# Up projection of a hybrid decoder layer: where the split weights of three of seven products begin in their buffers

## The chip, the cores and the metric

The kernel runs on one core of a Trainium2 chip. The metric is the device time of one execution in microseconds; lower is better. Runs of the kernel before stand beside runs of the changed one.

## The reference

One decoder layer: token mixing (gated linear attention and differential attention) and a gated MLP with a short causal convolution, each with an RMSNorm before and after. What matters here is the first product of the MLP, `h @ w_ffn_in`, with 512 tokens, 2048 inputs and 2 x 5632 outputs, all in float32:

```python
def conv_ffn(h, w_ffn_in, conv_w, conv_b, w_ffn_out):
    S = h.shape[1]
    up = h @ w_ffn_in
    a, b = up[..., :D_FF], up[..., D_FF:]
    a_pad = jnp.pad(a, ((0, 0), (CONV_W - 1, 0), (0, 0)))
    a = (conv_w[0] * a_pad[:, 0:S] + conv_w[1] * a_pad[:, 1:S + 1]
         + conv_w[2] * a_pad[:, 2:S + 2] + conv_b)
    return (jax.nn.gelu(a, approximate=True) * b) @ w_ffn_out
```

## The kernel before

**Split products.** A float32 factor is split into a high part (a copy in the type float32r, on the scalar engine, L130) and a low part (the rest, by a subtraction on the vector engine, L131). Each product is then three matmuls: high weights by high tokens, high by low, low by high. `ah` and `al` hold the token operand's two parts; `whi` and `wlo` hold those of a granule of weights of 1024 numbers in each partition.

**Where a granule begins.** `halves()` takes the two parts from buffers of 1024 + 64 numbers, three in rotation for each part, and returns 1024 of them, from `place_w[0]` on: 0, or 16 numbers, which are 64 bytes. All tiles that TensorE reads here (`ah`, `al`, the sums below, `whi`, `wlo`, and the spare buffers `xhi`, `xlo`) begin at whole multiples of 128 bytes, and the matmuls step through them in pieces of 128 numbers, which are 512 bytes. So the place of an operand within 128 bytes is 0, but for weights where `place_w[0]` is 16: there it is 64.

**The stages.** The input projections and the attention heads come first, then the output projection of the mixer and the change to the MLP (`to_ffn`), which already does the first columns of the up projection (`mm_t`, L166 to L168) with half the tokens (256 columns) at a time: its `weights_f` sets `place_w[0]` to 16 for weights in `whi` and `wlo`, and 0 for those in the spare buffers. Then the rest of the up projection and the down projection run as fast matrix multiplications by blocks, with seven products for each 2x2 block of blocks in place of eight.

**The up projection.** It has 20 units: 10 groups of 512 columns in each of the two branches. A unit (`up_unit`) makes seven products, called `x0`, `z0`, `y0`, `z1`, `x1`, `y1`, `y2` by the PSUM chain that they add to, and each takes one token operand: `a11`, `s5`, `s2`, `s3`, `a12`, `s7`, `a22` in this order. `a11`, `a12`, `s7` and `a22` are four quarters of `ah` and `al` (`s7` takes the place of the quarter that is not needed any more): the four token operands. `s5`, `s2` and `s3` are tiles of their own: the three sums. `Unit.run` does one product: two granules, each split by `granule`, and then `up_prods`, which for each of two pieces of 128 columns and four pieces of 128 inputs makes the three matmuls of L920, L921 and L922, with 128x128 weights as the stationary operand and 256 token columns (two runs of 128) as the moving one. So a granule is 24 matmuls, a product 48, a unit 336, and the projection 6720. In the loop over units the next unit's `x0` stands ahead of this one's `y2`, so that in the order of the program a run of three products on sums (144 matmuls) is followed by a run of four on token operands (192 matmuls).

The down projection uses the same class with `a == 2` and the place 0; there the tokens are the stationary operand (`down_prods`).

What sets the order is the order written out in the loop over units, with a scheduler that places the instructions of each engine; TensorE works its queue in order.

Of the kernel before, what the change touches and what calls it, by code (L numbers as in the profile page):

```python
# [35 lines left out]
def hybrid_layer(ctx: ExitStack, tc: tile.TileContext, x, attn_pre_norm, w_in, w_alpha_up, b_alpha,  # L36
# [69 lines left out]
    place_w = [0]  # L106
# [14 lines left out]
    def granule(src, a, raw=None, spare=None, hl=None):  # L121
        if raw is None:
            raw = load(src, a)
        if hl is not None:
            hi, lo = hl[:, 0, :], hl[:, 1, :]
        elif spare:
            hi, lo = spare_halves(spare)
        else:
            hi, lo = halves()
        act(hi, raw, AF.Copy)  # L130
        tt(lo, raw, hi.bitcast(F32), ALU.subtract)  # L131
        r = "p (a b) -> p a b"
        return hi.rearrange(r, a=a), lo.rearrange(r, a=a)
# [718 lines left out]
    class Unit:  # L852
# [4 lines left out]
        def run(self, seg, op, raws):  # L857
            c = seg[0]
            if seg[1] == "0":
                self.banks[c] = self.chain(c)  # L860
            for g in range(2):
                turn[0] += 1
                place_w[0] = 16 if self.a == 4 else 0
                hl = granule(None, self.a, raws[g], spare=extra[0] and turn[0] % 4 == 0)
                self.prods(self.banks[c], op, g, hl, seg[1] == "0")

# [354 lines left out]
```

## Time and profile before

| what | value |
|---|---|
| three runs | 2157.59, 2170.23, 2169.51 us |
| their median | 2169.51 us |
| the profiled execution | 2165.04 us |
| its span, first to last instruction | 2163.3 us |
| granted clock of TensorE, mean | 0.998 |
| stage of the up projection, us from the span's start | 926.8 to 1723.1 |

The profiled execution's own time is 1.7 us over its span. In the rows of groups, "xN | busy, mean ns" gives the number of instructions, the time in which at least one of them ran, and the mean length of one. Matmuls overlap, so the mean length of one is longer than the distance between their starts. A row of the matmuls in order of time begins with the start and the length in us. In the rows by stage a pair such as "795.71 (x6746)" is an engine's busy time and the number of its instructions that ran in the stretch, those that began before it among them.

### The profile page before, as it was taken

To read this page: it belongs to the slowest core of one execution; us is meant where nothing else is said; L and a number is where in the kernel's file an instruction comes from. 1 tells how busy PE (TensorE), PEld (TensorE's weight loads), DVE (VectorE), ACT (ScalarE), POOL (GpSimd) and SP (SyncE) were. 2 spreads that over 40 slices of the span, in tenths; PEclk is the share of its full clock that TensorE was granted. 3 is DMA by queue.
4 is the path that set the end of the run, shared out by engine and by line. 5 is a ranking of instruction groups with operands and counts; after the bars stand their busy time and mean duration, and the time that the engine had idled before them with its cause. 6 is when DMAs were issued, how large, how long until landed. Compare 5 with 4: busy or idle time off the path is not lost.

```text
span 2163.3 us, 31876 instructions
## 1 busy us (share of the span) xinstructions
PE 2133.1 (99%) x13009; PEld 1902.4 (88%) x13009; DVE 1418.1 (66%) x1722; ACT 901.7 (42%) x1162; POOL 204.9 (9%) x245
## 2 busy tenths in 40 slices
PE   7999999999999999999999999999999999999997
PEld 6878888888888889899999999999999978887886
DVE  5345553444444236787777677786777787888987
ACT  4233332333333234344444444543544555443533
POOL 1000000000000000011101101111111011111101
PEclk9999999999999999999999999999999999999999
DMA  6322222223224344455666657657667688577663
GB/s 212 104 69 78 78 73 84 69 78 87 78 88 166 98 136 170 132 127 136 161 163 154 159 147 180 157 129 184 147 143 184 182 243 217 166 193 177 158 173 136
DMA packets 218472, 303.83 MB, mean 140 GB/s; under 512 B 11777, under 2 KB 155573, under 8 KB 216405
## 3 DMA queue, kind: packets, MB, share of 16 engines
q1 hardware_dynamic: 165204, 238.87, 33.1%
q0 software_dynamic: 53120, 62.92, 18.9%
q8 instruction: 102, 1.67, 0.3%
q14 instruction: 46, 0.37, 0.0%
HBM read 273.97 MB, written 27.79 MB: 139 GB/s over the span
## 4 chain that ended last, share of the span: by engine, by line
PE 62%; issue 29%; POOL 3%; DVE 2%; DMA 2%; ACT 1%; SPq 0%; POOLq 0%; DVEq 0%; ACTq 0%
PE bank L184 6%; PE bank L185 6%; PE bank L186 6%; PE bank L920 5%; PE bank L922 5%; PE bank L921 5%; PE bank L168 5%; PE bank L166 5%; PE bank L167 5%; PE bank L1018 2%; PE bank L1019 2%; PE bank L1017 2%; POOL rt L869 1%; POOL raw L869 1%; PE bank L434 1%
## 5 line engine op out<-in xcount | busy, mean ns | idle before, releaser
L131 DVE TENSOR_TENSOR wlo<-raw,whi 128x1024 fp32r<-128x1024 f32 x307 | 374.3, 1221 | 360.4 <-ACT whi L130 352.6
L130 ACT ACTIVATE whi<-raw 128x1024 fp32r<-128x1024 f32 x307 | 324.9, 1059 | 599.1 <-PE bank L186 158.0
L922 PE MATMUL bank<-ah,wlo 128*128 128x256 f32 x1280 | 359.4, 281 | 0.6 <-DVE wlo L131 0.6
L920 PE MATMUL bank<-ah,whi 128*128 128x256 f32 x1280 | 359.2, 281 | 0.0
L921 PE MATMUL bank<-al,whi 128*128 128x256 f32 x1280 | 359.2, 281 | 0.0
L131 DVE TENSOR_TENSOR wlo<-rt,whi 128x1024 fp32r<-128x1024 f32 x221 | 269.1, 1221 | 105.2 <-ACT whi L130 105.1
L130 ACT ACTIVATE whi<-rt 128x1024 fp32r<-128x1024 f32 x221 | 233.3, 1059 | 241.2 <-PE bank L921 177.7
L922 PEld LDWEIGHTS bank<-ah,wlo 128*128 128x128 f32 x1280 | 242.9, 190 | 0.9 <-DVE wlo L131 0.8
L921 PEld LDWEIGHTS bank<-al,whi 128*128 128x128 f32 x1280 | 242.7, 190 | 0.1
L920 PEld LDWEIGHTS bank<-ah,whi 128*128 128x128 f32 x1280 | 240.3, 188 | 0.1
L184 PE MATMUL bank<-whi,ah 128*128 128x512 f32 x600 | 236.6, 397 | 0.5 <-ACT ah L143 0.5
L185 PE MATMUL bank<-wlo,ah 128*128 128x512 f32 x600 | 235.5, 393 | 0.0
L186 PE MATMUL bank<-whi,al 128*128 128x512 f32 x600 | 234.7, 393 | 0.0
L166 PE MATMUL bank<-ah,whi 128*128 128x512 f32 (+1 forms) x512 | 196.0, 383 | 0.0
L168 PE MATMUL bank<-ah,wlo 128*128 128x512 f32 (+1 forms) x512 | 194.6, 380 | 0.0
L167 PE MATMUL bank<-al,whi 128*128 128x512 f32 (+1 forms) x512 | 194.4, 380 | 0.0
L1018 PE MATMUL bank<-wlo,ah 128*128 128x512 f32 x424 | 166.2, 392 | 1.2 <-DVE wlo L131 1.1
L1019 PE MATMUL bank<-whi,al 128*128 128x512 f32 x424 | 165.7, 391 | 0.0
L1017 PE MATMUL bank<-whi,ah 128*128 128x512 f32 x424 | 156.7, 391 | 2.7 <-ACT whi L130 2.4
L186 PEld LDWEIGHTS bank<-whi,al 128*128 128x128 f32 x600 | 113.1, 188 | 24.2 <-DVE al L144 0.3
L185 PEld LDWEIGHTS bank<-wlo,ah 128*128 128x128 f32 x600 | 113.1, 189 | 23.7 <-DVE wlo L131 0.5
L184 PEld LDWEIGHTS bank<-whi,ah 128*128 128x128 f32 x600 | 113.0, 189 | 23.7 <-ACT ah L143 0.9
(259 smaller groups left out, 4080.0 us busy)
## 6 DMA issues: line engine op xcount, KB each, us to landing
raw<-in_w_in_dram SPq DMA_DIRECT2D x96, 512.0 KB, 3.7
raw<-in_w_ffn_in_dram SPq DMA_DIRECT2D x96, 512.0 KB, 4.6
raw<-in_w_ffn_out_dram SPq DMA_DIRECT2D x48, 512.0 KB, 6.2
rt<-in_w_ffn_in_dram SPq DMA_DIRECT2D x40, 512.0 KB, 5.6
rt<-in_w_ffn_in_dram POOLq DMA_DIRECT2D x40, 512.0 KB, 6.2
raw<-in_w_ffn_in_dram POOLq DMA_DIRECT2D x40, 512.0 KB, 7.1
raw<-in_w_o_dram SPq DMA_DIRECT2D x32, 512.0 KB, 3.8
rt<-in_w_ffn_out_dram SPq DMA_DIRECT2D x20, 512.0 KB, 6.3
```

The costliest lines, as they stand in the source:

```text
L130: act(hi, raw, AF.Copy)
L131: tt(lo, raw, hi.bitcast(F32), ALU.subtract)
L166: mm(o, wh, ah[:, t0:t1, kk, :], start=st, stop=False)
L167: mm(o, wh, al[:, t0:t1, kk, :], start=False, stop=False)
L168: mm(o, wl, ah[:, t0:t1, kk, :], start=False, stop=sp)
L184: mm(banks[t], ah[:, t, s, :], w[0][:, k, :], start=st, stop=False)
L185: mm(banks[t], ah[:, t, s, :], w[1][:, k, :], start=False, stop=False)
L186: mm(banks[t], al[:, t, s, :], w[0][:, k, :], start=False, stop=sp)
L920: mm(o, wh, sh[:, :, kk, :], start=start and kk == 0 and n == 0, stop=False, **NOW)
L921: mm(o, wh, sl[:, :, kk, :], start=False, stop=False, **NOW)
L922: mm(o, wl, sh[:, :, kk, :], start=False, stop=kk == HK - 1, **NOW)
L1018: mm(b[j], sh[:, o:o + P], w[1][:, q, :], start=False, stop=False, **NOW)
```

## The change

`Unit.run` sets the place of the weights by the product's token operand. For `a11`, `a12`, `a22` and `s7` in the up projection it stays 16 numbers, 64 bytes. For `s5`, `s2` and `s3` it is 0. Buffers, instructions, waits and their order on every engine stay the same; the addresses of the split's output and of the stationary operand differ in the three products on sums.

```diff
@@ Unit.run
             for g in range(2):
                 turn[0] += 1
-                place_w[0] = 16 if self.a == 4 else 0
+                place_w[0] = 16 if self.a == 4 and op in ("a11", "a12", "a22", "s7") else 0
                 hl = granule(None, self.a, raws[g], spare=extra[0] and turn[0] % 4 == 0)
                 self.prods(self.banks[c], op, g, hl, seg[1] == "0")
```

## The prediction

> **What bounds the kernel now.** I read the page's busy table first, then the busy times by stage, then what TensorE waited for, then TensorE's matmuls in order of time.
>
> ```profile
> span 2163.3 us, 31876 instructions
> PE 2133.1 (99%) x13009; PEld 1902.4 (88%) x13009; DVE 1418.1 (66%) x1722; ACT 901.7 (42%) x1162; POOL 204.9 (9%) x245
> 926.80:1723.10 796.30, 795.71 (x6746) 794.17 (x6745) 596.37 (x603) 375.05 (x409) 102.57 (x80) 1.00 0.67 158
> PE bank L922 <- DVE wlo L131: 0.6, 1, 0.6
> ```
>
> The first two lines are the whole program, the third is the stretch of the up projection (its columns: PE, PEld, DVE, ACT, POOL, granted clock, DMA share, GB/s), the fourth is the only wait of TensorE that the profile lists inside that stretch. TensorE is busy for 795.71 of 796.30 us there, at a granted clock of 1.00, and waits 0.6 us. The vector engine is busy for 596 us and the scalar engine for 375 us, so both have slack. In this stage the time is the number of matmuls multiplied by the distance from one matmul's start to the next one's. The "mean ns of one" in the rows of groups is longer than that distance, because matmuls overlap, so I take distances from starts.
>
> **Which matmuls the change touches.** Per line (L920, L921, L922) the groups of that stretch show 1280 matmuls on the four token operands and 320 on each of the three sums:
>
> ```profile
> L920 PE MATMUL bank<-ah,whi 128*128 128x256 f32 x1280 | 359.2, 281 | 0.0
> L920 PE MATMUL bank<-s5h,whi 128*128 128x256 f32 x320 | 89.8, 281 | 0.0
> L922 PE MATMUL bank<-s2h,wlo 128*128 128x256 f32 x320 | 89.9, 281 | 0.0
> L921 PE MATMUL bank<-s3l,whi 128*128 128x256 f32 x320 | 89.8, 280 | 0.0
> ```
>
> The change moves the weights of 3 sums x 3 lines x 320 = 2880 matmuls from 64 bytes past a 128-byte line to its start. 3 x 1280 = 3840 matmuls keep their place. All moving operands (`ah`, `al` and the sums) begin at whole multiples of 128 bytes, so "place" means the start within 128 bytes. Today both groups stand at 64 and both cost the same, 281 and 280 to 281 ns a record, so a sum's tile differs from a token operand's in nothing that the rows show.
>
> **What a matmul costs at either place.** The up projection of today has only the one place, but the stage ahead of it (`to_ffn`) has both, with the same 128x128 weights and the same 256 moving columns out of `ah` and `al`: `whi`/`wlo` there begin 64 bytes in (`weights_f` without a spare), `xhi`/`xlo` begin at 0 (with one). Matmuls in order of time around one run of each:
>
> ```profile
> 857.90 0.28 PE L166 MATMUL bank<-ah,whi 128*128 128x256 f32 x1
> ...
> 866.26 0.28 PE L168 MATMUL bank<-ah,wlo 128*128 128x256 f32 x1
> 866.38 0.28 PE L166 MATMUL bank<-ah,xhi 128*128 128x256 f32 x1
> ...
> 877.78 0.28 PE L168 MATMUL bank<-ah,xlo 128*128 128x256 f32 x1
> 877.90 0.28 PE L166 MATMUL bank<-ah,whi 128*128 128x256 f32 x1
> ```
>
> By the program's order the first run is 3 granules of 24 matmuls, 72 of them, with 71 distances: (866.26 - 857.90) / 71 = 117.75 ns. The second is 4 granules, 96 matmuls and 95 distances: (877.78 - 866.38) / 95 = 120.0 ns. Nothing else separates the two runs but the place and the tile's name. The groups inside the two runs say the same of the single record, 281 against 283 ns:
>
> ```profile
> L168 PE MATMUL bank<-ah,wlo 128*128 128x256 f32 x23 | 6.5, 281 | 0.0
> L168 PE MATMUL bank<-ah,xlo 128*128 128x256 f32 x31 | 8.8, 283 | 0.0
> ```
>
> The long stretch of the up projection without a stall gives the distance for place 64 more sharply. By the program's order the matmul at 1274.90 is the 2954th from 927.10:
>
> ```profile
> 927.10 0.28 PE L920 MATMUL bank<-ah,whi 128*128 128x256 f32 x1
> ...
> 1274.90 0.28 PE L921 MATMUL bank<-al,whi 128*128 128x256 f32 x1
> 1275.11 0.39 PE L922 MATMUL bank<-ah,wlo 128*128 128x256 f32 x1
> ```
>
> (1274.90 - 927.10) / 2953 = 117.78 ns, with operands and sums mixed. So a matmul at the same place costs 120.0 - 117.78 = 2.22 ns more.
>
> **The sum.** 2880 x 2.22 ns = 6.4 us, all on the path that sets the end, since TensorE waits for nothing. The bounds for this term are 0 (the place is without effect on sums) and twice it, 12.8 us (as if the sums' other stride, 4 KiB between their two runs of 128 columns against 8 KiB in `ah`, doubled the cost); a gain would need the short state of the second rival. I take 6.4, because the row it comes from has the same widths, the same engine order and the same place.
>
> A second term is the state that TensorE's two streams fall into. In one stretch of the up projection the distance is smaller at the same place:
>
> ```profile
> 1297.97 0.38 PE L922 MATMUL bank<-s2h,wlo 128*128 128x256 f32 x1
> 1298.19 0.28 PE L920 MATMUL bank<-s2h,whi 128*128 128x256 f32 x1
> ...
> 1352.38 0.28 PE L921 MATMUL bank<-al,whi 128*128 128x256 f32 x1
> 1353.25 0.38 PE L922 MATMUL bank<-ah,wlo 128*128 128x256 f32 x1 [0.59 <-DVE wlo L131]
> L920 PE MATMUL bank<-ah,whi 128*128 128x256 f32 x88 | 24.3, 276 | 0.0
> L920 PE MATMUL bank<-s3h,whi 128*128 128x256 f32 x32 | 8.8, 276 | 0.0
> ```
>
> From 1298.19 to 1352.38 there are 479 matmuls by the program's order: 54.19 / 478 = 113.4 ns, and the records shrink from 281 to 276 ns. The stretch begins at a matmul that had come late (1297.97) and ends at the next that came late (1353.25). It saves 479 x 4.4 ns = 2.1 us in this execution. After the change the place alternates in each unit, so such a stretch would end at the next sum. I expect that it is lost: +2.1 us.
>
> The work of the other engines that the edit touches is the split of each granule, whose output moves by 64 bytes. The rows for place 64 (up) and place 0 (the down projection) are alike, and both are hidden behind TensorE:
>
> ```profile
> L130 ACT ACTIVATE whi<-rt 128x1024 fp32r<-128x1024 f32 x160 | 169.6, 1060 | 192.4 <-PE bank L921 177.7 <-DMA rt<-in_w_ffn_in_dram 6.0 <-PE bank L167 4.4
> L130 ACT ACTIVATE whi<-rt 128x1024 fp32r<-128x1024 f32 x59 | 61.6, 1054 | 46.1 <-DMA rt<-in_w_ffn_out_dram 26.3 <-PE bank L1019 15.0 <-DVE rt L885 4.9
> L131 DVE TENSOR_TENSOR wlo<-rt,whi 128x1024 fp32r<-128x1024 f32 x160 | 195.4, 1221 | 81.1 <-ACT whi L130 81.1
> L131 DVE TENSOR_TENSOR wlo<-rt,whi 128x1024 fp32r<-128x1024 f32 x59 | 71.2, 1220 | 24.1 <-ACT whi L130 24.0
> ```
>
> 1060 against 1054 ns and 1221 against 1220 ns: nothing. ACT waits mostly for TensorE to free a buffer (177.7 us), so if the cover were gone, 120 granules x 6 ns would be under 1 us. No instruction, wait or DMA is added or moved.
>
> Made against the profiled execution's own 2165.04 us the sum is 2165.0 + 6.4 + 2.1 = 2173.5 us. The median of the three runs is 2169.51, 4.5 us above that execution, and two of the three lie near 2170, which I read as runs with little or no short-distance stretch (an estimate): 2169.5 + 6.4 = 2175.9. I predict 2175.0, between the two, 0.25 to 0.4% slower.
>
> **The rivals.** (1) *The place does nothing here.* The Trainium skill speaks for it: "TensorE: Matmul & The Clock Gate", in "Step-by-step: what each phase is for", says that the streaming operand and the weight load have read ports of their own, so that loading the next weights takes no read bandwidth from the running matmul. By that rule the change costs nothing. The trace of this case disagrees: 117.75 against 120.0 ns in two neighbouring runs. As a mechanism of this kernel the rival is that the 2.22 ns belongs to the `x` tiles and not to their place, or that the sums, which are other tiles than `ah`, are immune. Price: 2165 to 2169.5 us.
>
> (2) *The alternation puts the streams into the short state, faster.* The short state exists at place 64, and it was entered at a disturbance of the order. If each return from the sums to the four token operands set it, 3840 matmuls would gain 4.4 ns, 16.9 us, less about 1 us of gain that is there already, against the 6.4 us and 1 us lost on sums: 2165 - 16 + 7.5 = 2156.5, -0.4%. If the sums ran so too, 6720 - 479 = 6241 matmuls x 4.4 ns = 27.5 us: 2137.5, -1.3%. Against it: `to_ffn` makes the same return twice, at 857.90 and 877.90, and the run from 857.90 went on at 117.75 ns; and the matmuls of `to_ffn` at place 0 took 283 ns, not 276.
>
> (3) *The alternation spoils the four token operands as well, more slowly than forecast.* If the streams came out of the sums in the state of place 0 and stayed there, all 6720 matmuls would cost 120.0 ns: 6720 x 2.22 = 14.9, with 2.1 lost, 2182 us (2186.5 from the median), +0.8%. Against it stands the same return at 857.90.
>
> **How the numbers follow.** Forecast 0.72; no effect 0.09; faster by the short state in the token operands 0.06, in all 0.03; all at 120 ns 0.10. The three runs before lie 0.6% apart, and 1% is about what a measurement of this kernel can tell from no change. The forecast and the no-effect case lie within 1% but for a run-to-run spread, to which I give 0.02 beyond the upper bound and 0.01 beyond the lower; the third rival lies near the upper bound, and I give half of it, 0.05, to slower; of the second I give 0.03 plus 0.01 to faster. To stay honest about unknown effects of place I add 0.03 to slower and 0.02 to faster. That makes faster 0.07, within 1% 0.83, slower 0.10. The range of 8 in 10 reaches from 2162 (the no-effect case on a quick run) to 2185 (between the two values of the third rival).
>
> **What would show it.** In the profile after, L920 to L922 on the sums should have records of 283 ns, on `ah` and `al` still 281; a run of 144 matmuls on sums should take 17.3 us from start to start and the next 192 on token operands 22.6 us; the up projection's stretch should be 8 us longer, at 804 to 805 us. The forecast is wrong if the sums stay at 281 ns (rival 1), if records of 276 ns fill the token operands' runs (rival 2), if 283 appears there (rival 3), or if TensorE begins to wait for `wlo`.

## The result and the profile after

| | median | runs | from to |
|---|---|---|---|
| before | 2169.15 us | 20 | 2157.59 to 2172.16 |
| changed | 2173.81 us | 20 | 2169.72 to 2179.04 |

The ratio is 1.0029, 95% interval 1.0021 to 1.0037: the changed kernel is slower, by 4.7 us between the medians and by 6.3 us by the ratio, well inside 1%. The groups of the changed kernel's matmuls, for the stretch of the up projection:

```profile
L920 PE MATMUL bank<-ah,whi 128*128 128x256 f32 x1280 | 359.8, 281 | 0.0
L920 PE MATMUL bank<-s5h,whi 128*128 128x256 f32 x320 | 90.5, 283 | 0.0
L922 PE MATMUL bank<-s2h,wlo 128*128 128x256 f32 x320 | 90.6, 283 | 0.0
L921 PE MATMUL bank<-s3l,whi 128*128 128x256 f32 x320 | 90.5, 283 | 0.0
```

The four token operands stayed at 281 ns a record, and the three sums went from 280 or 281 to 283. In order of time, around the first run of sums and the run of token operands behind it:

```profile
934.32 0.28 PE L920 MATMUL bank<-s5h,whi 128*128 128x256 f32 x1
...
951.48 0.28 PE L922 MATMUL bank<-s3h,wlo 128*128 128x256 f32 x1
951.60 0.28 PE L920 MATMUL bank<-ah,whi 128*128 128x256 f32 x1
...
974.10 0.28 PE L922 MATMUL bank<-ah,wlo 128*128 128x256 f32 x1
974.22 0.28 PE L920 MATMUL bank<-s5h,whi 128*128 128x256 f32 x1
```

144 matmuls on sums take 951.60 - 934.32 = 17.28 us, 120.0 ns each from start to start. The 192 on token operands take 974.22 - 951.60 = 22.62 us, 117.8 ns each. Over the whole projection the mean distances are 119.98 ns (2880 matmuls) and 117.76 ns.

The profiled execution of the changed kernel took 2177.86 us, 4 us over its median, and so differs from the one before by 12.8 us. The starts split that:

```profile
928.67 0.28 PE L920 MATMUL bank<-ah,whi 128*128 128x256 f32 x1
...
1731.91 0.28 PE L922 MATMUL bank<-ah,wlo 128*128 128x256 f32 x1
PE bank L1017 <- ACT whi L130: 4.1, 5, 1.6
PE bank L1018 <- DVE wlo L131: 2.5, 5, 0.6
```

The up projection, from its first matmul to its last, took 803.24 us, against 796.01 (927.10 to 1723.11) before: 7.2 us. It began 1.6 us later, and 4.0 us came behind it. In the down projection TensorE waited 6.6 us for split weights in these two rows, where it had waited 3.5 before; those parts have the same code in both kernels. That the change has no hand in them was not shown, but the medians of 20 runs differ by 4.7 us, not by 12.8.

### The profile page after: what moved, and what is told of

It is laid out like the page before. It is cut to its first block, busy times and chain, and to the rows that moved or that the text cites. A ratio compares the mean times of both kernels' runs of the same rounds, so it can differ in the third digit from the quotient of the medians.

```text
span 2176.2 us, 31876 instructions
## 1 busy us (share of the span) xinstructions
PE 2142.5 (98%) x13009; PEld 1909.4 (88%) x13009; DVE 1418.0 (65%) x1722; ACT 900.9 (41%) x1162; POOL 204.7 (9%) x245
## 4 chain that ended last, share of the span: by engine, by line
PE 80%; issue 13%; DVE 2%; DMA 2%; POOL 1%; ACT 1%; SPq 0%; POOLq 0%; DVEq 0%; ACTq 0%
PE bank L920 12%; PE bank L921 12%; PE bank L922 12%; PE bank L185 6%; PE bank L184 6%; PE bank L186 6%; PE bank L168 5%; PE bank L166 5%; PE bank L167 5%; PE bank L434 1%; PE bank L1018 1%; PE bank L1017 1%; PE bank L1019 1%; PE bank L502 1%; PE bank L533 1%
## 5 line engine op out<-in xcount | busy, mean ns | idle before, releaser
L185 PEld LDWEIGHTS bank<-wlo,ah 128*128 128x128 f32 x600 | 113.3, 189 | 23.7 <-DVE wlo L131 0.5
```

Of the source, the lines that this page charges most:

```text
L185: mm(banks[t], ah[:, t, s, :], w[1][:, k, :], start=False, stop=False)
```

## The experiments

All distances below are from one matmul's start to the next one's, within a product, from the trace of the one profiled execution. Three steady values come back again and again, and each goes with one length of the record: 113.3 ns (276 in the rows of groups), 117.8 ns (281) and 120.0 ns (283). A product is called irregular where its distances step up and down and have only a mean; its records then can have a mean length that looks like one of the three (281 for `s5` at 118.4 ns below). Times and ratios stand against runs of the kernel before on the same chip in the same series.

**All products at place 0, and the change turned round.** Do the 2.2 ns belong to the place, or to the alternation of places, or to the sums' tiles?

```diff
 # e2_all0
-                place_w[0] = 16 if self.a == 4 else 0
+                place_w[0] = 0
 # e3_swap
-                place_w[0] = 16 if self.a == 4 else 0
+                place_w[0] = 16 if self.a == 4 and op in ("s5", "s2", "s3") else 0
```

> All seven products at place 0, no alternation. Theory (each matmul at the same place costs 2.22 ns more): 6720 x 2.22 = 14.9 us over before, about 8.5 us over the changed kernel, ratio to before 1.007; all matmuls 120.0 ns from start to start. Rival (the change of place from run to run costs, not the place): within 1 us of before, ratio 1.000.

> The change turned round: token operands at place 0, sums at 64; it alternates as often as the changed kernel. Theory: 3840 x 2.22 = 8.5 us over before, ratio 1.004; token operands 120.0 ns, sums 117.8. Rival (alternation costs): the same as the changed kernel, 1.003, with no difference between the groups. Rival (the cost belongs to the sums' tiles): no change, 1.000.

With all at 0: median 2180.61 us against 2165.31, ratio 1.0072 (1.0059 to 1.0084). Turned round: 2175.94 us, ratio 1.0042 (1.0029 to 1.0056). Rows of the two, in this order:

```profile
L920 PE MATMUL bank<-ah,whi 128*128 128x256 f32 x1280 | 362.3, 283 | 0.0
L920 PE MATMUL bank<-s5h,whi 128*128 128x256 f32 x320 | 90.6, 283 | 0.0
```

```profile
L920 PE MATMUL bank<-ah,whi 128*128 128x256 f32 x1280 | 362.3, 283 | 0.0
L920 PE MATMUL bank<-s5h,whi 128*128 128x256 f32 x320 | 89.9, 281 | 0.0
```

All 283 in the first; in the second the token operands have 283 and the sums 281. So the price goes with the place, on whichever tile, and adds up by the number of matmuls: 2880, 3840 and 6720 of them gave 1.0029, 1.0042 and 1.0072. Alternation is not what costs: the kernel without any is the slowest, and the turned one needs no term for it (3840 x 2.22 = 8.5 us worked out, 9.1 by the ratio).

**The sums' tiles moved by 64 bytes.** Does the weights' own place count, or its relation to the moving operand's?

```diff
 # e7_shift
+    shift = ctx.enter_context(tc.tile_pool(name="shift", bufs=1)).tile([P, 16], F32, name="shift")
+    nc.gpsimd.memset(shift, 0.0)
     fp = ctx.enter_context(tc.tile_pool(name="fp", bufs=2))
...
-                place_w[0] = 16 if self.a == 4 else 0
+                place_w[0] = 16 if self.a == 4 and op != "s3" else 0
```

> A 64-byte tile ahead of the pool puts the tiles of the three sums 64 bytes past a multiple of 128; buffers of the weights are as before. Weights at 64 for all products but s3, whose weights begin at 0. So s5 and s2 stand at the same place (64, 64), s3 apart (0 against 64), token operands apart (64 against 0). Theory (the relation counts): s5 and s2 120.0 ns from start to start, s3 117.8 (or 113.4, if the entry puts it into the short state). Rival (the place of the weights alone counts): s5 and s2 117.8, s3 120.0.

One run took 2168.49 us. The rows of the up projection:

```profile
L920 PE MATMUL bank<-ah,whi 128*128 128x256 f32 x1280 | 359.7, 281 | 0.0
L920 PE MATMUL bank<-s5h,whi 128*128 128x256 f32 x320 | 90.5, 283 | 0.0
L920 PE MATMUL bank<-s2h,whi 128*128 128x256 f32 x320 | 90.6, 283 | 0.0
L920 PE MATMUL bank<-s3h,whi 128*128 128x256 f32 x320 | 88.7, 277 | 0.0
```

`s5` and `s2`, with weights at 64 and the moving operand at 64, ran at 119.9 and 120.0 ns. `s3`, weights at 0 and moving operand at 64, ran at 115.4 in the mean: 113.3 in its first granule and about 117.8 from where the scheduler puts two matmuls of the next product between. The place of the weights alone would have given 117.8, 117.8 and 120.0. So it is the relation of the two places that counts, and for `s3` the run shows that two different places have two states. The step from `s2` to `s3` in one unit:

```profile
1024.39 0.28 PE L921 MATMUL bank<-s2l,whi 128*128 128x256 f32 x1
1024.51 0.28 PE L922 MATMUL bank<-s2h,wlo 128*128 128x256 f32 x1
1024.63 0.28 PE L920 MATMUL bank<-s3h,whi 128*128 128x256 f32 x1
1024.74 0.28 PE L921 MATMUL bank<-s3l,whi 128*128 128x256 f32 x1
1024.86 0.28 PE L922 MATMUL bank<-s3h,wlo 128*128 128x256 f32 x1
```

`s2` had stepped steadily at 120 ns ahead of it, and still `s3` took the short state at once, as it did in each unit. The token operands of the changed kernel took 117.8 behind sums at 120.0. There the weights begin 64 bytes after the moving operand's place, here 64 before it.

**Seven places in one kernel.**

```diff
 # e1_map
-                place_w[0] = 16 if self.a == 4 else 0
+                place_w[0] = {"a11": 0, "a22": 4, "s5": 8, "s2": 16, "s3": 24, "a12": 32, "s7": 48}[op] if self.a == 4 else 0
```

> Each of the seven products of the up projection has a place of its own for its weights, in bytes: a11 0, a22 16, s5 32, s2 64, s3 96, a12 128, s7 192; the moving operands begin at whole multiples of 128 bytes. Read from start to start of its matmuls. Theory (a matmul is dearer when the weights that load beside it begin at the same place within 128 bytes as the moving operand): a11 and a12 120.0 ns, s2 and s7 117.8 ns; 16, 32 and 96 bytes are not known, between 117.8 and 120.0. Rival (only the place within the buffer counts, 0 against anything else): a12 117.8 too. Rival (the alternation of places within a unit is what costs): all products near 120.0.

One run took 2171.49 us. The rows of the three sums:

```profile
L920 PE MATMUL bank<-s5h,whi 128*128 128x256 f32 x320 | 89.9, 281 | 0.0
L920 PE MATMUL bank<-s2h,whi 128*128 128x256 f32 x320 | 88.4, 276 | 0.0
L920 PE MATMUL bank<-s3h,whi 128*128 128x256 f32 x320 | 90.1, 282 | 0.0
```

Mean distances: `a11` (0 bytes) 119.9, `a22` (16) 118.3, `s5` (32) 118.4, `s2` (64) 113.5, `s3` (96) 118.9, `a12` (128) 118.6, `s7` (192) 117.8 ns. At 16 and 32 bytes the matmuls have no steady distance but an irregular pattern, mostly between 115 and 123 ns. The theory held for `a11` and `s7`, and failed in two places: `a12`, at 128 bytes, which by the theory is the same place as the moving operand, was not at 120.0 but irregular, and `s2`, at 64 bytes, was not at 117.8 but at 113.5, short in every unit but the first. What stands ahead of those two is another product that is not steady at 117.8 or 120.0. One reading is that the place decides which states there are, and the product ahead decides which of them is taken. It does not cover everything: `s7`, at 192 bytes, stands behind the irregular `a12` and stayed at 117.8 in all 20 units. And for `a12` there is a rival that no run separates: that 128 bytes apart is not the same place. In the built programs of the kernel before and of this one, every weight buffer and every token tile begins at a whole multiple of 256 bytes, so places within 128 and within 256 bytes are alike for all products but `a12` and `s7`, and just these two do not fit.

**The sums moved with narrower weight buffers.** The question is that of `e7_shift`, but more than the places is changed.

```diff
 # e4_moving
-        return [wpool.tile([P, GR + 64], F32R, name=n, tag=n)[:, sl] for n in ("whi", "wlo")]
+        return [wpool.tile([P, GR + 32], F32R, name=n, tag=n)[:, sl] for n in ("whi", "wlo")]
...
-        return fp.tile([P, D], dt, name=name, tag="t8", bufs=6)
+        return fp.tile([P, D + 32], dt, name=name, tag="t8", bufs=6)[:, at:at + D]
...
-        up[n] = tuple(large_tile(f"{n}{v}", F32R).rearrange("p (t k c) -> p t k c", t=2, k=HK) for v in "hl")
+        up[n] = tuple(large_tile(f"{n}{v}", F32R, 0 if n == "s3" else 16).rearrange("p (t k c) -> p t k c", t=2, k=HK) for v in "hl")
...
-                place_w[0] = 16 if self.a == 4 else 0
+                place_w[0] = 16 if self.a == 4 and op not in ("s5", "s3") else 0
```

> The tiles of s5 and s2 begin 64 bytes in, those of s3 at 0; the weights begin at 0 for s5 and s3 and at 64 for s2 and for the four token operands. Theory (the relation of the two places counts): s5 117.8 ns from start to start (weights 0, moving 64), s2 120.0 (64, 64), s3 120.0 (0, 0), token operands 117.8 (64, 0). Rival (the place of the weights alone counts): s5 120.0, s2 117.8, s3 120.0. Rival (sums are dearer than token operands by their stride): all three alike at 120.0.

One run took 2170.83 us. To make room, the buffers of the weights had to shrink by 128 bytes, so that their starts lie elsewhere in all stages: the up projection began only at 940.50 us. All three sums were irregular (118.7, 118.0, 117.9 ns), which fits neither theory. The trace has a hint of the cause: the means of the granules of `s5` come back every three units (121.2 and 117.8, then 117.5 and 120.0, then 117.5 and 117.7), and with 14 granules a unit and three buffers in rotation, the same buffer comes back every three units too. A buffer was 4352 bytes, 17 x 256, and here is 4224, 16.5 x 256, so that here neighbouring buffers lie 128 bytes apart within 256. If only the place within 128 bytes counted, the buffer could not matter. This speaks for the rival named with `a12`; no run tests it alone. The token operands behind them, with weights at 64 as before, were at 113.4 to 114.7 ns:

```profile
L920 PE MATMUL bank<-ah,whi 128*128 128x256 f32 x1280 | 353.8, 276 | 0.0
```

Here too, 64 bytes took the short state behind an irregular product.

**One granule at 32 bytes in each unit.** If the state is taken at the entry, a short irregular run should bring the whole projection into the short one.

```diff
 # e6_kick
-                place_w[0] = 16 if self.a == 4 else 0
+                place_w[0] = (8 if op == "s5" and g == 0 else 16) if self.a == 4 else 0
 # e8_kick0
-                place_w[0] = 16 if self.a == 4 else 0
+                place_w[0] = (16 if op[0] == "a" or op == "s7" else 8 if op == "s5" and g == 0 else 0) if self.a == 4 else 0
```

> As before, with all weights of the up projection at 64, but for the first granule of s5 in each unit, which begins at 32 bytes: 480 of the 6720 matmuls. Theory (at 64 bytes there are two steady states, 113.3 and 117.8 ns, and which one is taken depends on the state from which the run is entered; from the irregular state at 32 bytes it is the short one, which then lasts until the next late matmul): some 5800 to 6200 matmuls x 4.4 ns = 25 to 27 us less, ratio 0.988. Rival (the short state of s2 in the run with seven places came from 32 bytes in both granules and from what stood ahead of them): 117.8 ns stay, ratio 1.000.

> The changed kernel, with the first granule of s5 in each unit at 32 bytes in place of 0. If 120.0 ns belong to the same place as such, the sums but for that granule stay at 120.0, and only the token operands can gain: rival, ratio 1.003 as the changed kernel. Theory (the state is entered from what stood ahead): sums go on irregularly at about 118 ns, and token operands fall to 113.4: 3840 x (117.8 - 113.4) = 17 us less than the changed kernel minus 2880 x 2 = 5 us, so 16 us under before, ratio 0.993.

With all else at 64 (`e6_kick`) the profiled execution did what the theory says:

```profile
L920 PE MATMUL bank<-ah,whi 128*128 128x256 f32 x1280 | 353.6, 276 | 0.1
L920 PE MATMUL bank<-s2h,whi 128*128 128x256 f32 x320 | 88.3, 276 | 0.0
```

It took 2144.29 us. But the median of its 12 runs is 2165.33 against 2166.62, ratio 0.9983 (0.9963 to 1.0002), with runs from 2144.29 to 2168.93 and nine of the twelve over 2165. Only the quickest has a trace; by their times, the others mostly did not go short. On top of the changed kernel (`e8_kick0`) the ratio to before is 1.0018 (1.0009 to 1.0027), and the sums came back to 120.0 ns within the second granule of `s5`. There my expectation of 0.993 was wrong: in all units but the first, the same place did not keep the irregular pattern, and the token operands behind the steady sums ran at 117.8, but for four granules of one unit behind a late matmul. In the first unit the sums had 120.0 only as the mean of a repeating 120, 120, 125, 117 and 118, and the token operands behind them had the short state.

**A whole product at 32 bytes.**

```diff
 # e10_kick2
-                place_w[0] = 16 if self.a == 4 else 0
+                place_w[0] = {"a22": 4, "s5": 8}.get(op, 16) if self.a == 4 else 0
 # e11_kick1
-                place_w[0] = 16 if self.a == 4 else 0
+                place_w[0] = {"s5": 8}.get(op, 16) if self.a == 4 else 0
```

> All weights of the up projection at 64 bytes but for a22 at 16 and, right behind it in the program, s5 at 32, both whole products, as in the run with seven places, where s2 behind them was at 113.4 ns in all 20 units. Theory (behind a run in the irregular state, 64 bytes takes the short state, in each unit and in each execution): s2, s3, a12, s7 and a11, 4800 matmuls, at 113.4 ns, 21 us less, a22 and s5 at 118.4, 1 us more: ratio 0.991 in the middle, with executions that lie close together. Rival (whether the short state is taken is left to the execution): executions spread as with the single granule at 32 bytes, from 0.990 to 1.001, most at 1.000.

> All weights of the up projection at 64 bytes but for s5, both granules, at 32. Theory (the irregular state at 32 bytes is enough, if it lasts a whole product): 5760 matmuls at 113.4 ns, 25 us less, 960 at 118.4, 0.6 us more: ratio 0.989. Rival (the entry from 64 bytes leaves a regular pattern that comes back to 117.8 at the end of s5): 1.000.

`a22` at 16 and `s5` at 32: 2151.24 us against 2168.51, ratio 0.9918 (0.9904 to 0.9932), runs from 2147.16 to 2152.74. `s5` alone: 2142.95 us, ratio 0.9893 (0.9875 to 0.9910), runs from 2141.68 to 2149.17. Both came out as worked out ahead (0.991 and 0.989), and the second beats the kernel before. Its rows, and its entry into the short state in the second unit:

```profile
L920 PE MATMUL bank<-ah,whi 128*128 128x256 f32 x1280 | 354.0, 277 | 0.0
L920 PE MATMUL bank<-s5h,whi 128*128 128x256 f32 x320 | 89.9, 281 | 0.0
L920 PE MATMUL bank<-s3h,whi 128*128 128x256 f32 x320 | 88.4, 276 | 0.0
```

```profile
978.01 0.28 PE L920 MATMUL bank<-s2h,whi 128*128 128x256 f32 x1
978.13 0.28 PE L921 MATMUL bank<-s2l,whi 128*128 128x256 f32 x1
978.25 0.28 PE L922 MATMUL bank<-s2h,wlo 128*128 128x256 f32 x1
978.37 0.28 PE L920 MATMUL bank<-s2h,whi 128*128 128x256 f32 x1
978.48 0.28 PE L921 MATMUL bank<-s2l,whi 128*128 128x256 f32 x1
978.60 0.28 PE L922 MATMUL bank<-s2h,wlo 128*128 128x256 f32 x1
978.71 0.28 PE L920 MATMUL bank<-s2h,whi 128*128 128x256 f32 x1
```

After a few matmuls at 0.12 us the distances go to 0.11 to 0.12, that is to 113.3, and stay there until the next `s5`. In the first unit of both kernels `s5` was irregular too, but the products behind it ran at 117.8. So an irregular product ahead is not enough by itself. One thing that differs there is the order: the scheduler puts two matmuls of `s2` ahead of the last 22 of `s5`. Whether that is the reason was not tested.

**64 bytes in the other stages too.**

```diff
 # e5_all64
-    place_w = [0]
+    place_w = [16]
...
-            place_w[0] = 0 if spare else 16
...
-            place_w[0] = 0
...
-                place_w[0] = 16 if self.a == 4 else 0
...
-    place_w[0] = 0
```

> The split weights begin 64 bytes in everywhere in the program, so also in the input projections, the output projection and the down projection, whose matmuls have 512 moving columns and 227 ns from start to start before. Theory (same place costs about 2.2 ns a matmul whatever its length): some 4600 matmuls x 2.22 = 10 us less than before, ratio 0.995, about 224.4 ns each. Rival (with 512 columns the weight load is hidden and the place does nothing): 1.000, 227 ns.

2159.65 us against 2166.62 in the medians, ratio 0.9978 (0.9952 to 1.0005), and the runs lie far apart, from 2151.95 to 2179.44 us. The profiled execution was one of the long ones, 2179.35 us, and in it the matmuls with 512 columns were longer than at place 0. One group, before and here:

```profile
L166 PE MATMUL bank<-ah,whi 128*128 128x512 f32 x448 | 178.0, 397 | 0.0
L166 PE MATMUL bank<-ah,whi 128*128 128x512 f32 x448 | 180.2, 402 | 0.0
```

The mean distance of this group was 233.4 ns; over the lines with 512 columns the means are 228 to 233, where they were 227 to 228 before. So the expectation of 224.4 was wrong for this execution; what the short ones did was not seen. This stays open: with 512 columns 64 bytes is not simply the better place.

## Why the prediction was right, point by point

- *What bounds the kernel* held: with all products at 0 the up projection was 15.7 us longer in the profiled execution than before, and the whole 17.3; with `s5` at 32 bytes it was 19.5 shorter, and the whole 22.1. The rest of an execution moves by some microseconds of its own, 5.6 of the 12.8 us in the changed kernel.
- *The cost of the place*, 2.22 ns, was right: 119.98 - 117.76 = 2.22 ns in the changed kernel. That it is right to the hundredth is luck: its 120.0 came from 95 distances between two starts that were read to 0.01 us, which leaves 0.1 ns, and the neighbouring run at 64 alone would have given 2.25. The experiments with all at 0 and with the places changed round confirm the count of matmuls as the factor.
- *The lost short stretch* held as far as it can be seen: the changed kernel's profile has such matmuls only in the last granules, behind a late one. The up projection grew by 7.2 us, to 803.24 and so a little less than the 804 to 805 that were to show it, against the 8.5 us of the two terms. Late matmuls explain most of the rest: they cost 1.3 us in the execution before (three times) and 0.2 in the one after, and 8.5 - 1.1 = 7.4. In the runs without a trace the second term does not show: the change costs 4.7 us in the medians and 6.3 by the ratio, no more than the 6.4 us of the first term alone. The forecast of 2175.0, between the values with and without the second term, lies 1.2 us over the measured median.
- *Rival 1, no effect*, is out. The Trainium skill's "TensorE: Matmul & The Clock Gate", "Step-by-step: what each phase is for", has it that loading the next weights takes no read bandwidth from the running matmul. That the place then costs nothing, as the rival had it, the trace does not bear out: 2.22 ns a matmul between two places, and 6.7 between the best state and the worst. Whether it is the reads that get into each other's way, no run shows.
- *Rival 2, the short state by alternation*, did not come, and the return in `to_ffn` had spoken against it: behind sums at 120.0 ns the token operands, with weights at 64, go to 117.8. But its mechanism is real: a return can set the short state. It does behind `s5` at 32 bytes in all units but the first, and that kernel is 1.07% faster than before; with the places the other way (weights 0, moving operand 64) it did even behind products at 120.0 ns.
- *Rival 3*, all at 120 ns, did not come in the changed kernel. Its price from the median, 2186.5, is 2.1 us too high by the forecast's own reading, in which the median has no short stretch to lose: 2169.5 + 14.9 = 2184.4.
- *A detail of the order* was not as told: the scheduler puts two matmuls of the next product ahead of the last 22 of `s3` in most units, so the runs are 122, 2, 22 and 190 long. In the changed kernel this matters little (the last 22 of `s3` are at 119.7 to 120.0), but in the run with the sums moved by 64 bytes `s3` went from 113.3 to 117.8 at those two matmuls, and stayed at 113.3 in the one unit without them.
- The single step that was weaker than it sounded was the sentence that a matmul at the same place costs 120.0 ns. It did in `to_ffn`, in the change and with all at 0. In the map of seven places `a12`, at the same place within 128 bytes, took 118.6, either because of what stood ahead of it or because 128 bytes apart is not the same place.

## What to carry to other kernels

Where TensorE is the bound and each matmul brings its own weights, take the distance from start to start, not the length of the record, and compare it between places of the stationary and the moving operand: here 113.3, 117.8 and 120.0 ns for the same 128x128 by 256 matmul. An older stage of the same kernel that has both variants is the best price list for a change of addresses. Where a stage shows two distances at the same addresses, look for what selects them; here one product at an odd place in each unit kept nearly all the rest in the quick state, and that was worth nearly four times as much as the change itself (1.07% against 0.29%).

## What the runs showed of the hardware that was not expected

- The relation of the two places sets the possible distances, and what came before chooses among them: 120.0 at the same place (weights 0 and moving 0, or 64 and 64); 117.8 or 113.3 when they are 64 bytes apart; irregular, 118.3 to 118.4 in the mean, at 16 or 32 bytes apart. After how many bytes the relation repeats was not tested; `a12` at 128 bytes and the pattern of the run with narrower buffers speak against 128.
- What chooses is known only in part. Weights 64 bytes after the moving operand's place went short behind an irregular product in most cases, but not in the first unit; `s7` at 192 did not in any unit; weights 64 bytes before it went short behind products at 120.0.
- A state can last for hundreds of matmuls, over changes of the tile (479 in a row in the trace of before). A late matmul can end it but need not: of the three late places in the trace of before, two changed the state, and in the quick traces with `s5` at 32 bytes (one granule, or the product) the short state went on behind late matmuls near 1188 and 1342 us, the latest of them 0.9 us late.
- Executions of one kernel spread widely: 2144.29 to 2168.93 us with one granule at 32 bytes. That the state makes this difference is likely (the quickest was short almost throughout), but the others have no trace, and why the same program should take one state in one execution and the other in the next was not settled.
